# Layer 0's last twelve convolution tiles as six pairs of seven products, with part of the weights' low halves made by accumulating DMAs

## The chip, the cores and the metric

The kernel runs on one core of one Trainium2 chip. The metric is device time in microseconds for one execution. The kernel before took 2328.89 us (median of 3 runs, 2328.8 to 2331.57).

## What is computed

The reference is one inference step of a two-layer trunk, D = 2048, for 128 prompt tokens and 512 sample tokens (640 in all). Each layer normalises x, scales and shifts it by adaLN values (h), multiplies h by one wide input projection, runs two mixers on slices of the result, and adds the output projection's result, gated, to x. Layer 0's second mixer is the short gated convolution of this case:

```python
def gated_short_conv(u, gate_b, gate_c, w):
    z = gate_c * u
    zp = jnp.pad(z, ((0, 0), (1, 1), (0, 0)))
    conv = zp[:, :-2] * w[0] + zp[:, 1:-1] * w[1] + zp[:, 2:] * w[2]
    return gate_b * conv

def modulation(cond, w, b):
    m = jax.nn.silu(cond) @ w + b
    return jnp.split(m, 3, axis=-1)
...
y_b = gated_short_conv(ub, bb, cb, conv_w) * jax.nn.silu(gb)
return jnp.concatenate([y_a, y_b], axis=-1) @ w_out
```

ub, bb, cb and gb are four slices of 1024 columns of the layer's input projection h @ w_in, 6656 columns wide.

## The kernel before

**Numbers.** Every product is made of three matmuls in a rounded 32-bit type: a value is split into a high half (the rounded value) and a low half (the rest), and high by high, high by low and low by high are summed. `split` (lines 240 to 242) makes the high half with an ACT copy and the low half with a DVE subtraction. Weights are loaded as `raw`, 128 x 512 (four blocks of 128 rows of k), and split by `split_w` (line 259) into `wh` and `wl`; there are four buffers each (`W_BUFS`).

**Tiles.** A tile is 128 output columns by all 640 tokens. It goes through sixteen blocks of k in four quarters, and the tokens in two halves of 320 (`proj_q`, lines 270 to 278): 16 x 2 x 3 = 96 matmuls. `run_tiles` runs 52 such tiles for layer 0's input projection. The first six ("leading" tiles) run together while h is made block by block (`h0_maker`, lines 889 to 901; ACT's line 897 writes the high half) and while adaLN weights for layer 0, in 2 MB DMAs, go through TensorE (line 178). The other 46 follow, first those for attention (k, v, q, gates) with the convolution tiles of i = 0 to 3 between them, then sixteen convolution tiles, u, c, b and h for each i = 4 to 7 (`b_tiles`), of which no attention is left beside.

**Slots and fills.** After each quarter `slot` advances a step of attention and, at a given rate, a step of a fill: `ada_on_dve` (lines 194 to 229) computes the other adaLN blocks on DVE, 16 steps a block, each a load of 256 KB and two DVE instructions (line 213). `fill0` does twelve blocks at 1.2 steps a slot.

**Pairs.** `run_pairs` (from line 431) takes two tiles at once as a two-by-two block product (k in halves, tokens in halves) with seven half-tile products, in the order Q1, Q2, N5, P6, P7, P4, Q3. Each product is 8 blocks of k x 3 = 24 matmuls (lines 526 to 528) on sums of weight blocks, formed by `operand` on DVE in a tile `sx` (lines 462, 465, 472), and on sums of token blocks (T1 to T4), formed before by `forms` (lines 1050 to 1074) from the mixer outputs in memory. Weight parts are split three parts ahead (`SPLIT_AHEAD`); a part is half a product, 12 matmuls. Here the pairs serve the output projections alone: `project_out` (line 1098) runs three leading tiles, one single tile, and six pairs for layer 0.

**Order.** Each engine works in its own order, which the tile framework sets when the program is built; buffers and semaphores do the rest. Mixer outputs go to memory by DMAs that POOL issues (line 827), and the residual's transpose too (line 909). SP issues the loads.

Of the kernel before, what the change touches and what calls it, by code (L numbers as in the profile page):

```python
# [15 lines left out]
ALU = mybir.AluOpType  # L16
# [29 lines left out]
SPLIT_AHEAD = 3  # L46
N_FILL0 = 12
FILL0 = 1.2
FILL1 = 0.9
# [4 lines left out]
def trunk_kernel(ctx: ExitStack, tc: tile.TileContext, I: dict, O: dict):  # L54
# [136 lines left out]
    def ada_on_dve(blocks, tags, parts=1, tie=lambda: None):  # L191
# [4 lines left out]
        for l, cb in blocks:  # L196
# [34 lines left out]
            yield  # L231

    ready = set()

# [22 lines left out]

    mark = [None]
# [39 lines left out]

    credit = [0.0]

    def slot(fill=None, rate=0.0):
        advance(prep, len(prep))
        advance(attn, 1)
        credit[0] += rate
        while credit[0] >= 1.0:
            next(fill, None)
            credit[0] -= 1.0

    def run_tiles(jobs, w_ap, make_h, fill=None, rate=0.0, ahead=None, order=(0, 1, 2, 3), before=None,
                  last=None, by_half=False, trans=[], grace=0, cut=None, summed=None, led=None, fill_from=0, lead_in=None):  # L310
        if trans:
            lp = tc.tile_pool(name="lead", bufs=1, side="right")
            lead_pool = lp.__enter__()
            sums = {n: lead_pool.tile([P, NT], F32, name=f"sum{n}") for n in trans}
            held = [n for n in range(2 + len(trans)) if n not in trans]

            leads = [n for m in range(len(held) + 1) for n in trans[m:m + 1] + held[m:m + 1]]
            leads += trans[len(held) + 1:]
        else:
            leads, held, lp = list(range(min(3, len(jobs)))), [], None  # L320
# [4 lines left out]
        for ui, (pos, qd, js) in enumerate(units):  # L325
            raws = {n: load_raw(w_ap, jobs[n][0], qd, js) for n in leads[:W_BUFS]}
# [66 lines left out]
        if before:  # L393
            settle()
        else:
            n = pending.pop(0)
            begin(jobs[n][1], pps[n])
        for i in range(lead, len(jobs)):
# [3 lines left out]
            for qd in range(4):  # L402
                proj_q(pp, parts[t], qd, qd, HV[:1] if split_last else HV)
                if before and qd == 0:
                    before(i)
                t += 1
                run_ahead(t)
                if pending and not prep:
                    n = pending.pop(0)
                    begin(jobs[n][1], pps[n])  # L410
                slot(fill, rate if t > fill_from else 0.0)
            if split_last:
# [17 lines left out]

    def run_pairs(cols, w_ap, mov, room, begin, part, done, tail):

# [22 lines left out]
        def operand(p, name):  # L455
# [3 lines left out]
            if name == "N5":  # L459
                x = st8["x"] = ap.tile([P, W8, P], F32, tag="sx", name="sx", bufs=1)  # L460
                for i in range(2):
                    V.tensor_add(halves(x)[i], halves(a("A21"))[i], a("A22")[i])
                return halves(x)
            if name == "P6":
                V.tensor_add(st8["x"], st8["x"], a("A11"))
# [24 lines left out]
        def after(p, name, ps):  # L490
# [8 lines left out]
            elif name == "P6":  # L499
                V.tensor_sub(u2, ps, q1)  # L500
                V.tensor_sub(u4, st8["n5"], u2)
                if p == len(cols) - 1:
                    part(p, 0, 1, u4)
            elif name == "P7":
                V.tensor_sub(z, ps, u4)
                done(p, 1, 1, z)
                V.tensor_add(u2, ps, u2)
                part(p, 1, 0, u2)
            elif name == "P4":
                done(p, 1, 0, ps)  # L510
            elif p == len(cols) - 1:
                done(p, 0, 1, ps)
# [7 lines left out]
        for i, (p, name) in enumerate(seq):  # L520
            ps, rows_ = pproj.tile([P, 512], F32, tag=f"p{'ab'[i % 2]}{i // 2 % 2}", name="pq")[:, 0:HALF], mov[MOV[name]]
            for h in range(2):
# [6 lines left out]
                if h == 0:  # L529
                    ahead(2 * i + 1)  # L530
                    slot()
            after(p, name, ps)
# [8 lines left out]
            if name in ("P6", "P7") and p == len(cols) - 1:  # L541
                tail(name)
            slot()

# [198 lines left out]
    def pair_gen(ap, width, k, banded, emit, done, sinks):  # L743
# [35 lines left out]
        for u in range(6):  # L779
# [12 lines left out]
            if u < 5:  # L792
# [21 lines left out]
    fill0 = ada_on_dve(ada_rest[:N_FILL0], ("acc0", "acc1", "adaw", "adaw", "adaw", "z"))  # L814
    fill1 = ada_on_dve(ada_rest[N_FILL0:], ("acc0", "acc1", "adaw", "adaw", "adaw", "adaw"), 2,
                       lambda: mark[-1])
# [3 lines left out]
    xdram = [dram.tile([P, NT], F32, name=f"xd{k}") for k in range(KT)]  # L820

# [83 lines left out]
    def keep(ui, n, pp):  # L905
        g = {(4, 0): 0, (4, 4): 1, (5, 0): 2, (5, 4): 3}.get((ui, n))
        if g is not None:
            V.tensor_copy(xTm[g][:, 4 * NT:], pp[1][:, 0:1])
            nc.gpsimd.dma_start(x0dram[g], xTm[g])

    def even_start():
        close("start")
        open_pool("even")


# [98 lines left out]
    for i in range(4):  # L1014
# [29 lines left out]

    def forms():

        f = None

        def load(j):
            ts = [big("w8", bufs=4)[:, 0:NT] for _ in range(2)]  # L1050
            for i in range(2):
                nc.sync.dma_start(ts[i], ydram[j + 8 * i])
            return ts
# [4 lines left out]
        for j in range(8):  # L1058
            (ya, yb), nxt = nxt, (load(j + 1) if j < 7 else None)
            b11, b12, b21, b22 = ya[:, 0:HALF], ya[:, HALF:NT], yb[:, 0:HALF], yb[:, HALF:NT]  # L1060
            x = big("sx")[:, 0:3 * HALF]
# [3 lines left out]
            x2, x3, x4 = (x[:, i * HALF:(i + 1) * HALF] for i in range(3))  # L1065
            V.tensor_sub(x3, b12, b22)
            V.tensor_sub(x2, b11, x3)
            V.tensor_sub(x4, b21, x2)
            V.tensor_sub(d, b11, b12)
            t = big(f"T{j}", dtype=F32R).rearrange("p (s n) -> p s n", s=2)  # L1070
            split(t[:, 0, :], t[:, 1, :], x)
            T.append(t)
# [22 lines left out]
    def form_of(i):  # L1095
        return lambda j: (T[j][:, 0, i * HALF:(i + 1) * HALF], T[j][:, 1, i * HALF:(i + 1) * HALF])

    def project_out(l, maker, finish, last, tail):

        w = W_OUT[l]  # L1100

        def job(n):
            def f(pp):
                res_load(l, n)
                for i in range(2):
                    res_sum(l, n, pp[i], CS[:1] if i == 0 else CS[1:])
                yield
                finish(n)
            return f

        n0 = N_SINGLE[l]
        go_on = run_tiles([(n * P, job(n)) for n in range(3)], w, maker, order=(0, 2, 1, 3))


        quarters = [(n * P, qd) for n in range(3, n0) for qd in range(4)]
        raws, parts = [], []
# [8 lines left out]
        go_on()  # L1125
        for n in range(3, n0):
            pp, t = new_pp((n - 3) % 2), 4 * (n - 3)
            for hv in ([HV] if n < n0 - 1 else [HV[1:], HV[:1]]):
# [10 lines left out]
            while n == n0 - 1 and go_on():  # L1139
                pass  # L1140
            drain(prep)
            prep.append(job(n)(pp))
            advance(prep, 1)

# [13 lines left out]
        def done(p, t, h, src):  # L1158
# [4 lines left out]
            elif n in seen:  # L1163
                prep.append(later(n))
            seen.add(n)

        run_pairs([(n * P, (n + 1) * P) for n in range(n0, KT, 2)], w,
                  {"B11": half_of(0, 0), "T1": half_of(0, 1), "B21": half_of(8, 0), "B22": half_of(8, 1),
                   "T2": form_of(0), "T3": form_of(1), "T4": form_of(2)}, room, begin, part, done, tail)
        drain(prep)  # L1170


    make_y0 = y_maker(("q0h", "q0l", "q1h", "q1l"), NT)
# [60 lines left out]
    def x1_tail(name):  # L1234

        for k in (range(0, 4) if name == "P6" else range(4, 6)):
            x1_back(k, big("w8", bufs=4) if k < 4 else big("sx" if k == 4 else "sf"))

# [3 lines left out]

    project_out(0, y0_maker, x1_done, x1_last, x1_tail)

    def h1_maker(k, hv):
        if k == 0 and hv[0][0] == 0:
            for g in range(3):
                t = big(f"T{g}")
                for i in range(3 if g < 2 else 2):
                    x1_back(6 + 3 * g + i, t, i)  # L1250
            for i in (14, 15):
                x1[i] = st["xr", i]
# [151 lines left out]
    def y1_maker(k):  # L1404
        if k == 4:
# [4 lines left out]
            open_pool("fin")  # L1410
            attn.append(forms())
        if k % 8 >= 4:
# [87 lines left out]
```

## Time and profile before

| | us |
|---|---|
| runs, median (lowest to highest) | 2328.89 (2328.8 to 2331.57) |
| profiled execution, own time | 2333.26 |
| its span | 2331.3 |
| layer 0: start and leading tiles | to about 175 |
| layer 0: tiles beside attention | to about 690 |
| layer 0: last sixteen convolution tiles | to about 912 |
| layer 0: output projection, leading and single tiles | to about 980 |
| layer 0: output projection, pairs | to about 1106 |
| layer 1 | to the end |

In the rows of the profile, PE is TensorE's matmuls, PEld its weight loads, DVE the vector engine, ACT the scalar engine, POOL the engine that also issues DMAs, and SP the one that issues the loads. A row of stretches gives each engine's busy time and its count of instructions, then TensorE's granted clock, the mean busy share of the 16 DMA engines and GB/s. A row of a timeline gives start, duration, engine, line, operation, output and input, and in brackets how long the engine had been idle before it and what ended that. L12 is line 12 of the kernel before.

### The profile page before, as it was taken

What the parts mean: (1) busy time and instruction counts of PE and PEld (TensorE: products, weight loads), DVE (VectorE), ACT (ScalarE), POOL (GpSimd) and SP (SyncE); (2) the same over time, 40 slices, a digit from 0 to 9 for tenths busy, and PEclk for the clock granted to TensorE, in tenths of its full rate; (3) what the DMA queues carried; (4) which work ended last, traced back from release to release, by engine and by line L of the source; (5) the groups of instructions that cost most, each with busy time, mean ns of one, the idle gap of its engine ahead of it and who ended that gap; (6) DMA issues with size and microseconds to landing.
All of it is one profiled execution on the core that took longest, in us unless ns stands there. A gap on an engine that the chain in (4) does not pass through costs nothing.

```text
span 2331.3 us, 41439 instructions
## 1 busy us (share of the span) xinstructions
PE 2286.6 (98%) x15988; PEld 2210.0 (95%) x15988; DVE 1572.5 (67%) x3196; ACT 929.2 (40%) x1935; POOL 133.0 (6%) x181
## 2 busy tenths in 40 slices
PE   7999999999999999999999999999999999999999
PEld 5699999999999999999999999999999999999999
DVE  4559886786876663988855755755756754567576
ACT  4235442433422222544554344444334444444343
POOL 1001000000000000000010100101000001000101
PEclk9999999999999999999999999999999999999999
DMA  9984545445355443844431422413423312128642
GB/s 315 354 267 131 162 116 170 139 119 169 116 180 162 151 139 114 277 142 128 160 98 53 135 82 72 143 52 100 118 72 95 104 46 82 46 74 270 181 122 70
DMA packets 390630, 321.96 MB, mean 138 GB/s; under 512 B 18402, under 2 KB 336368, under 8 KB 389920
## 3 DMA queue, kind: packets, MB, share of 16 engines
q1 hardware_dynamic: 382496, 288.98, 40.9%
q0 software_dynamic: 7216, 28.16, 3.3%
q8 instruction: 126, 2.06, 0.4%
q10 hardware_dynamic: 720, 2.16, 0.3%
q14 instruction: 72, 0.59, 0.1%
HBM read 290.79 MB, written 28.44 MB: 137 GB/s over the span
## 4 chain that ended last, share of the span: by engine, by line
PE 88%; DMA 4%; DVE 4%; ACT 2%; issue 1%; POOL 0%; SPq 0%; ACTq 0%; DVEq 0%; POOLq 0%
PE pa L276 10%; PE pb L277 10%; PE pb L276 10%; PE pb L278 10%; PE pa L277 10%; PE pa L278 10%; PE pq L526 4%; PE pq L528 4%; PE pq L527 4%; PE T L704 2%; PE S L716 1%; PE S L718 1%; PE S L717 1%; DMA yin<-yd 1%; PE T L178 1%
## 5 line engine op out<-in xcount | busy, mean ns | idle before, releaser
L241 ACT ACTIVATE wh<-raw 128x512 fp32r<-128x512 f32 (+1 forms) x490 | 303.1, 620 | 794.7 <-PE pb L277 655.3
L242 DVE TENSOR_TENSOR wl<-raw,wh 128x512 fp32r<-128x512 f32 (+1 forms) x490 | 330.8, 676 | 351.3 <-ACT wh L241 326.1
L276 PE MATMUL pa<-h,wh 128*128 128x320 f32 x1760 | 560.6, 319 | 4.5 <-ACT h L241 3.2
L277 PE MATMUL pa<-h,wh 128*128 128x320 f32 x1760 | 547.3, 312 | 1.8 <-DVE h L242 1.8
L278 PE MATMUL pa<-h,wl 128*128 128x320 f32 x1760 | 546.4, 310 | 0.0
L278 PE MATMUL pb<-h,wl 128*128 128x320 f32 x1760 | 545.4, 310 | 0.0
L276 PE MATMUL pb<-h,wh 128*128 128x320 f32 x1760 | 545.0, 310 | 0.0
L277 PE MATMUL pb<-h,wh 128*128 128x320 f32 x1760 | 544.8, 310 | 0.0
L213 DVE SCALAR_TENSOR_TENSOR acc<-adaw,sT,acc 128x512 f32<-128x512 f32 (+1 forms) x600 | 357.4, 639 | 13.1 <-DMA adaw<-in_ada_w 12.4
L276 PEld LDWEIGHTS pa<-h,wh 128*128 128x128 f32 x1760 | 331.9, 189 | 24.0 <-issue 14.7
L277 PEld LDWEIGHTS pa<-h,wh 128*128 128x128 f32 x1760 | 332.6, 189 | 6.3 <-DVE h L242 2.7
L278 PEld LDWEIGHTS pa<-h,wl 128*128 128x128 f32 x1760 | 332.1, 189 | 1.2 <-issue 1.2
L278 PEld LDWEIGHTS pb<-h,wl 128*128 128x128 f32 x1760 | 330.8, 188 | 2.1 <-issue 2.1
L276 PEld LDWEIGHTS pb<-h,wh 128*128 128x128 f32 x1760 | 330.6, 188 | 1.0 <-issue 0.4
L277 PEld LDWEIGHTS pb<-h,wh 128*128 128x128 f32 x1760 | 330.8, 188 | 0.2
L690 ACT ACTIVATE p<-S,nm,rq 128x768 f32<-128x768 f32 (+3 forms) x120 | 101.2, 844 | 114.8 <-DVE nm L685 81.1
L526 PE MATMUL pq<-h,wh 128*128 128x320 f32 x352 | 110.0, 313 | 0.4 <-DVE xr L1083 0.4
L527 PE MATMUL pq<-h,wh 128*128 128x320 f32 x352 | 108.8, 309 | 0.0
L528 PE MATMUL pq<-h,wl 128*128 128x320 f32 x352 | 108.4, 309 | 0.0
L683 DVE TENSOR_REDUCE nm<-S 128x1 f32<-128x768 f32 (+3 forms) x120 | 91.9, 766 | 16.1 <-PE S L718 14.9
L241 ACT ACTIVATE pth<-T 128x512 fp32r<-128x512 f32 (+1 forms) x132 | 65.9, 533 | 71.4 <-PE T L704 71.3
L527 PE MATMUL pq<-T,wh 128*128 128x320 f32 x264 | 81.4, 308 | 0.0
(303 smaller groups left out, 3382.5 us busy)
## 6 DMA issues: line engine op xcount, KB each, us to landing
raw<-in_od_w_in SPq DMA_DIRECT2D x208, 256.0 KB, 2.8
raw<-in_ev_w_in SPq DMA_DIRECT2D x196, 256.0 KB, 3.0
adaw<-in_ada_w SPq DMA_DIRECT2D x192, 256.0 KB, 3.0
ada<-in_ada_w SPq DMA_DIRECT2D x14, 2048.0 KB, 11.0
adaw<-in_ada_w SPq DMA_DIRECT2D x128, 128.0 KB, 2.3
yd<-y POOLq DMA_DIRECT2D x34, 320.0 KB, 2.8
yin<-yd SPq DMA_DIRECT2D x32, 320.0 KB, 4.8
w<-yd SPq DMA_DIRECT2D x32, 320.0 KB, 4.4
```

The source lines that it names most:

```text
L213: V.scalar_tensor_tensor(out=a, in0=w, scalar=sT[:, kt, c:c + 1], in1=a, op0=ALU.mult, op1=ALU.add)
L241: A.activation(hi, x, AF.Copy)
L242: V.tensor_sub(lo, x, hi)
L276: PE.matmul(ps, wh[:, i, :], hi[:, sl], start=(j == js[0] if alone else (pos == 0 and j == 0)), stop=False)
L277: PE.matmul(ps, wh[:, i, :], lo[:, sl], start=False, stop=False)
L278: PE.matmul(ps, wl[:, i, :], hi[:, sl], start=False, stop=(j == js[1] - 1 if alone else (pos == 3 and j == 3)))
L526: PE.matmul(ps, wh[:, j, :], hi, start=(h == 0 and j == 0), stop=False)
L527: PE.matmul(ps, wh[:, j, :], lo, start=False, stop=False)
L528: PE.matmul(ps, wl[:, j, :], hi, start=False, stop=(h == 1 and j == 3))
L683: V.tensor_reduce(nm, s, axis=AX.X, op=ALU.max, negate=True)
L690: A.activation(p[:, 0:n], s, AF.Exp, scale=rsc, bias=nm, accum_out=l)
L704: PE.transpose(t[:, i * P:(i + 1) * P], p, ident)
```

## The change

- Layer 0's input projection keeps 36 tiles in `run_tiles`. The last sixteen go through a new function `project`, split out of `project_out`: four single tiles (u, c, b, h of i = 4), then twelve tiles in six pairs (u with c, b with h). The pool "even" of attention closes before them, and "mid" opens there instead of inside the output projection.
- The pairs need the token blocks' forms. `whole_tokens` writes h to memory: for each of 16 blocks one DMA of the high half and one accumulating DMA of the low half, all issued on POOL. `forms` takes its source as an argument and works in place.
- `split_w` can leave the subtraction to a DMA: ACT writes the high half, ACT writes its negative into `wl`, and a DMA on POOL adds `raw` to it. Two splits of three go so in the tiles beside attention (`by_dma` = 3), one of two from the convolution tiles to the end of layer 0's output projection (`by_dma` = 2).
- In `run_pairs` N5's sum of weights is formed in place in the loaded block A21, and the sum for P7 is formed at N5 instead of at P6. The convolution's results go through `conv_put`, by token halves.
- `fill0` has ten blocks at 1.64 steps a slot; the two others go by half blocks (`ada_by_half`, two 128 x 256 DVE instructions a step) at 0.42 steps a slot in the new pairs and in layer 0's output pairs.
- The output projection's first four inputs come through the three `xr` buffers (`late_yin`), no longer through four buffers of the old pool.

```diff
-N_FILL0 = 12
-FILL0 = 1.2
+N_FILL0 = 10
+FILL0 = 1.64
+FILL0_PAIRS = 0.42
+FILL0_LATE = 0.42
...
     def split_w(raw):
         wh = wpool.tile(raw.shape, F32R, tag="wh", name="wh")
         wl = wpool.tile(raw.shape, F32R, tag="wl", name="wl")
-        split(wh, wl, raw)
+        turn[0] += 1
+        if by_dma[0] and turn[0] % by_dma[0]:
+            A.activation(wh, raw, AF.Copy)
+            A.activation(wl, wh, AF.Copy, scale=-1.0)
+            nc.gpsimd.dma_start(wl, raw, accum_op=ALU.add)
+        else:
+            split(wh, wl, raw)
...
             if name == "N5":
-                x = st8["x"] = ap.tile([P, W8, P], F32, tag="sx", name="sx", bufs=1)
+                f = st8["f"] = ap.tile([P, W8, P], F32, tag="sf", name="sf", bufs=1)
+                V.tensor_add(f, a("A11"), a("A21"))
+                x = st8["x"] = a("A21")
                 for i in range(2):
-                    V.tensor_add(halves(x)[i], halves(a("A21"))[i], a("A22")[i])
+                    V.tensor_add(halves(x)[i], halves(x)[i], a("A22")[i])
                 return halves(x)
             if name == "P6":
                 V.tensor_add(st8["x"], st8["x"], a("A11"))
-                f = st8["f"] = ap.tile([P, W8, P], F32, tag="sf", name="sf", bufs=1)
-                V.tensor_add(f, a("A11"), a("A21"))
                 return halves(st8["x"])
...
+    def whole_tokens():
+        for _ in range(30):
+            yield
+        for k in range(KT):
+            for s, how in zip(hs[k], ({}, {"accum_op": ALU.add})):
+                nc.gpsimd.dma_start(hdram[k], s, **how)
+                yield
+
     def even_start():
         close("start")
         open_pool("even")
+        by_dma[0] = 3
+        extra.append(whole_tokens())
...
-    for i in range(4, 8):
-        b_tiles(i)
...
+    close("even")
+    open_pool("mid")
...
+    by_dma[0] = 2
+    attn.append(forms(hdram))
+    project(I["ev_w_in"][0], [EV["ucbh"[n % 4]] + (4 + n // 4) * P for n in range(16)], 0, 4, None, conv_job,
+            lambda p: None, None, lambda p, t, h, src: conv_put(4 + 2 * p + t, h, src), lambda name: None,
+            fill_late, FILL0_PAIRS)
...
     def y0_maker(k):
-        if k < 4:
-            return make_y0(k)
         if k == 8:
-            close("even")
-            open_pool("mid")
-            st["acc"] = pools["cur"].tile([P, NT], F32, name="acc")
-            st["sq"] = pools["cur"].tile([P, NT], F32, name="sq")
-            attn.append(forms())
+            attn.append(forms(ydram))
         late_yin(k)
```

More of the change, by code (lines that the diff above doesn't have):

```diff
@@ L297, in drain, with slot @@
             advance(queue, 1)
-    credit = [0.0]
-    def slot(fill=None, rate=0.0):
+    credit, pace, extra = [0.0], [0.0], []
+    def slot(fill=None, rate=0.0, steps=1.0):
         advance(prep, len(prep))
-        advance(attn, 1)
+        advance(extra, 1)
+        pace[0] += steps
+        while pace[0] >= 1.0:
+            advance(attn, 1)
+            pace[0] -= 1.0
         credit[0] += rate
@@ L542, in run_pairs @@
                 tail(name)
-            slot()
+            slot(fill, rate)
     def stage(ap, pp):
@@ L1095, in form_of, with project @@
     def form_of(i):
[L1096 to L1115, printed above, removed]
+        return lambda j: tuple(T[j][:, s, (2 - i) * HALF:(3 - i) * HALF] for s in range(2))
+    def project(w, cols, leads, n0, maker, job, begin, part, done, tail, fill=None, rate=0.0):
+        go_on = run_tiles([(cols[n], job(n)) for n in range(leads)], w, maker, order=(0, 2, 1, 3)) if leads else slot
+        quarters = [(cols[n], qd) for n in range(leads, n0) for qd in range(4)]
         raws, parts = [], []
@@ L1165, in done @@
             seen.add(n)
[L1167 to L1173, printed above, removed]
+        project(W_OUT[l], [n * P for n in range(KT)], 3, n0, maker, job, begin, part, done, tail,
+                *((fill_late, FILL0_LATE) if l == 0 else ()))
```

164 lines of the change are left out of this document (131 added, 33 removed).

## Prediction

> **What bounds the kernel now.** I read the page's busy shares and its chain first, then busy time by stage.
>
> ```profile
> PE 2286.6 (98%) x15988; PEld 2210.0 (95%) x15988; DVE 1572.5 (67%) x3196; ACT 929.2 (40%) x1935; POOL 133.0 (6%) x181
> ...
> q0 software_dynamic: 7216, 28.16, 3.3%
> ...
> PE 88%; DMA 4%; DVE 4%; ACT 2%; issue 1%; POOL 0%; SPq 0%; ACTq 0%; DVEq 0%; POOLq 0%
> ```
>
> ```profile
> 38.00:175.00 137.00, 131.93 (x989) 107.39 (x990) 70.03 (x171) 43.52 (x100) 2.19 (x4) 0.98 0.90 308
> 175.00:690.00 515.00, 512.82 (x3647) 498.39 (x3646) 408.64 (x825) 202.98 (x454) 23.32 (x25) 1.00 0.48 143
> 690.00:897.00 207.00, 207.00 (x1427) 204.57 (x1426) 128.95 (x235) 42.70 (x76) 2.16 (x4) 1.00 0.49 147
> 980.00:1106.00 126.00, 125.56 (x855) 125.13 (x854) 107.69 (x179) 53.32 (x86) 5.40 (x10) 1.00 0.49 143
> ```
>
> The columns are PE, PEld, DVE, ACT, POOL busy time, TensorE clock, DMA share, GB/s. TensorE bounds every stage: layer 0's leading tiles (38 to 175 us), its tiles beside attention (to 690), the convolution tiles that the change takes up (to 897) and the paired output projection (980 to 1106). But the slack differs: in the lead the DMA share is 0.90, so two resources are nearly full; among the last convolution tiles DVE is at 62% and DMA at half.
>
> **The change, part by part.** The sum is made against the profiled execution, 2333.26 us (span 2331.3). The runs' median is 4.4 us lower, and I take 4.4 off at the end.
>
> *Matmuls removed.* A pair of tiles is eight half-tile products of 24 matmuls; seven do now. Six pairs: 6 x 24 = 144 matmuls of 128x320 fewer, which the built program's order confirms (12792 to 12648).
>
> ```profile
> 750.00:800.00 50.00, 50.00 (x346) 49.39 (x346) 34.37 (x62) 9.70 (x18) 0.00 (x0) 1.00 0.54 164
> ```
>
> 50 / 346 = 0.1445 us each: **-20.8 us**, all on the path, if nothing waits.
>
> *Low halves by DMA, in the pairs.* In the built order one weight part in two, always a product's first, gets its low half so: ACT writes the high half, ACT writes its negative, POOL issues a DMA that adds the raw weights. The same part of the old output projection shows the cover. The rows are ACT, then DVE, then PE, at layer 0's pairs; sx is the sum of weight blocks for the products N5 and P6.
>
> ```profile
> 1032.12 0.63 ACT L241 ACTIVATE wh<-sx 128x512 fp32r<-128x512 f32 x1 [1.13 <-PE pq L527]
> 1033.82 0.63 ACT L241 ACTIVATE wh<-sx 128x512 fp32r<-128x512 f32 x1 [0.44 <-PE pq L527]
> ...
> 1034.48 0.69 DVE L242 TENSOR_TENSOR wl<-sx,wh 128x512 fp32r<-128x512 f32 x1 [0.25 <-ACT wh L241]
> 1035.21 1.23 DVE L465 TENSOR_TENSOR sx<-sx,w 128x1024 f32<-128x1024 f32 x1
> 1037.21 0.69 DVE L242 TENSOR_TENSOR wl<-sx,wh 128x512 fp32r<-128x512 f32 x1 [0.78 <-ACT wh L241]
> ...
> 1040.81 0.31 PE L526 MATMUL pq<-T,wh 128*128 128x320 f32 x1
> 1040.95 0.31 PE L527 MATMUL pq<-T,wh 128*128 128x320 f32 x1
> 1041.10 0.31 PE L528 MATMUL pq<-T,wl 128*128 128x320 f32 x1
> ```
>
> At 1032.12 the first part of N5 is split, released by the matmul that gave its buffer back; at 1035.21 DVE adds a block to sx for P6, in place; P6's low half is ready at 1037.90, and TensorE first needs it at 1041.10. The cover is 3.2 us. In the new order that addition must also wait until N5's DMA has read sx, and P6's own low half needs a second DMA. With D for issue to landing: 1032.12 + 0.63 + 0.63 (negative copy, priced as the other ACT row) + D + 1.23 + 0.63 + 0.63 + D, with 0.1 of hand-over, ends at 1036.0 + 2D. It meets 1041.10 if D is 2.55; beyond that TensorE waits **2D - 5.1** in each of 12 pairs (six new, six of the output projection, which now uses the DMAs as well). DVE is in order: behind the waiting addition stand the part's next subtractions and the sums of finished products, and behind those on SP the next weight block's load. Parts outside this chain have 3 parts of 12 matmuls (5.3 us), less two ACT rows: 4 us for D.
>
> No accumulating DMA is in the trace. Its nearest rows are POOL's plain ones (KB each, us to landing):
>
> ```profile
> yd<-y POOLq DMA_DIRECT2D x34, 320.0 KB, 2.8
> ...
> xd<-xr POOLq DMA_DIRECT2D x16, 320.0 KB, 3.6
> ...
> out_y_sample<-ot POOLq DMA_DIRECT2D x15, 256.0 KB, 3.6
> ...
> out_new_c_k<-kg POOLq DMA_DIRECT2D x8, 64.0 KB, 1.9
> ```
>
> On the line through 64 KB and the faster 320 KB, 256 KB land in 2.6 us: the lower end. The accumulation also reads its destination: q0 moved 28.16 MB in 3.3% of 2331 us, 2.73 us per MB, so 0.7 us for another 256 KB, D = 3.3. The upper end is the same-size row plus that, 4.3. I take 3.3, since a second read is real work: 1.5 us a pair, **+18 us** (ends +1 and +42).
>
> The Trainium skill's page "DMA: Bandwidth & Descriptors" (section "Anatomy of one DMA — SWDGE (gpsimd) path") fits a GpSimd-issued DMA as 2.0 us plus its bytes at 436 GB/s, an estimate of 2.6 us here, and says nothing there of an accumulation's second read. By that price the pairs would cost 1 us, and the sum would be 17 lower. The faster row of 320 KB fits it; the same-size row, 3.6, doesn't.
>
> *Copies of h to memory.* 32 DMAs of 320 KB (16 of them accumulating) write the tokens' h for the later forms. The source issues them after 30 slots beside attention; but in the built order they stand first on POOL, ahead of the residual's stores, each waiting only for its h. POOL is empty then, so they run as h is made, in the lead:
>
> ```profile
> L897 ACT ACTIVATE h<-ht,mod x32: 385/558/728, 37.2 to 149.9; 128x512 fp32r<-128x512 f32 x16, 128x128 fp32r<-128x128 f32 x16
> ```
>
> ```profile
> POOL x0d L909 <- DVE xT L908: 129.4, 3, 115.3
> ...
> PE T L178 <- DMA ada<-in_ada_w: 4.3, 2, 3.3
> ```
>
> ```profile
> 38.00:60.00 22.00, 22.00 (x174) 18.98 (x175) 10.22 (x26) 8.81 (x23) 0.00 (x0) 0.92 0.86 298
> 60.00:80.00 20.00, 14.96 (x106) 7.52 (x105) 6.60 (x18) 4.06 (x8) 0.00 (x0) 0.91 1.07 387
> 80.00:105.00 25.00, 25.00 (x172) 17.09 (x171) 13.23 (x29) 6.33 (x12) 0.00 (x0) 1.00 0.92 323
> 105.00:130.00 25.00, 25.00 (x203) 21.43 (x200) 18.02 (x42) 10.79 (x22) 0.00 (x0) 1.00 0.97 309
> 130.00:165.00 35.00, 34.97 (x275) 32.44 (x274) 19.59 (x52) 8.96 (x20) 1.66 (x3) 1.00 0.73 250
> ```
>
> At 2.73 us per MB the 10.5 MB are 29 us of all 16 engines, 43 with the second read. Up to 130 us the engines have 4 us free of 92, and TensorE already waits for ada weights (60 to 80: 5.0 us idle). h 0 to 3, eight copies, 7 to 11 us, fall there: I charge 8. h 4 to 11, sixteen copies, 14 to 21 us, meet loads that run a buffer ahead while TensorE is full: I charge a quarter, 4. The last eight fit the free 9 us after 130. **+12 us**, ends 0 and +28 (everything over the free time).
>
> The same page (section "Issuing engines are not separate DMA queues") says that what POOL issues shares the 16 engines with SP's loads, which speaks against this part: by it the copies press on the lead; with a path of their own they would cost 0 and the sum be 12 lower. No row of before shows such a load beside SP's.
>
> *DVE beside attention.* Ten adaLN blocks go in 30 tiles' 120 slots at 1.64 steps a slot, not 1.2; two of three splits leave DVE.
>
> ```profile
> L213 DVE SCALAR_TENSOR_TENSOR acc<-adaw,sT,acc 128x512 f32<-128x512 f32 x261 | 185.7, 745 | 4.9 <-DMA adaw<-in_ada_w 4.4 <-DVE acc L213 0.4
> L242 DVE TENSOR_TENSOR wl<-raw,wh 128x512 fp32r<-128x512 f32 x118 | 81.2, 688 | 59.3 <-ACT wh L241 53.5 <-PE T L555 5.6
> ...
> 200.00:250.00 50.00, 49.80 (x364) 46.33 (x363) 47.95 (x108) 24.90 (x58) 3.84 (x3) 1.00 0.44 128
> ```
>
> A slot is 515 / 120 = 4.3 us, 11.7 in 50 us, a step two instructions: +0.44 x 11.7 x 2 x 0.745 = +7.6 us of DVE, -0.67 x 11.7 x 0.69 = -5.4. The fullest stretch goes from 47.95 to 50.2 of 50: **+1 us** (0 to +5); elsewhere there is room. ACT gains 80 x 0.63 = 50 us on 203 of 515: hidden. In the pairs DVE (107.69 of 126) loses seven splits a pair, 4.8 us, and gains 64 / 12 = 5.3 half-width ada steps, each two of these:
>
> ```profile
> L213 DVE SCALAR_TENSOR_TENSOR acc<-adaw,sT,acc 128x256 f32<-128x256 f32 x240 | 102.4, 479 | 7.6 <-DMA adaw<-in_ada_w 7.4
> ```
>
> That is 5.1 us, so nothing changes: it stays hidden under TensorE's 168 x 126/855 = 24.8 us a pair, and 3 us more of DVE work there would not.
>
> *Forms and seams.* The new forms' DVE work is eight rounds of four subtractions and a split, priced by the old forms:
>
> ```profile
> L242 DVE TENSOR_TENSOR T<-sx,T 128x960 fp32r<-128x960 f32 x16 | 18.5, 1158 | 3.7 <-ACT T L241 3.5
> ...
> L1068 DVE TENSOR_TENSOR sx<-w,sx 128x320 f32<-128x320 f32 x16 | 7.8, 487 | 0.2
> ```
>
> 8 x (4 x 0.49 + 1.16) = 25 us in the four single tiles' 4 x 96 x 0.1445 = 55, beside eight weight splits (5.5) and the convolution, with no ada: hidden; so are the 16 loads of 320 KB, 14 us of the engines' time at a share of one half. The first output tiles lose their four input buffers and go through three: **+2 us** (0 to +6).
>
> Sum: -20.8 + 18 + 12 + 1 + 2 = **+12**, 2345.5 on the profile's scale, **2341 us** in the runs' median.
>
> **Rivals.**
>
> *The cover holds (faster).* D is near 2.6 and the lead's loads run far enough ahead: -20.8 + 1 + 5 + 1 + 2 = -12, 2317 us. For it: the faster 320 KB row, 2.8, and a lead in which TensorE idles only 5 us of 137. Against: the second read, and a DMA share of 0.95 up to 130 us. It decides at D = 2.9 with a lead of 9: then 8 + 9 + 3 cancels the 20.8.
>
> *The ring of four weight buffers binds.* If D passes 4.3, even parts outside the chain are late: four parts take 7.04 us now; two ACT rows, D and the ten matmuls after the wait are 2.8 + D. At D = 5.3 that is 1.0 us per four parts, 42 times, and the chain's 5.5 a pair overlaps it; some 7 a pair, 84 in all: +78, 2407 us. For it: 3.6 for a plain 256 KB row, with half the engines' time already taken. Against: it needs two thirds more than that line gives.
>
> *Nothing measurable.* The terms cancel, as at the point above: 2329. That the change doesn't remove the matmuls is excluded by their count; that TensorE's time doesn't shrink is the forecast itself.
>
> **How the numbers follow.** A measurement tells about 0.2%, 4.7 us, from no change. Forecast, 2334 to 2382: 0.53. Cover holds, below 2324: 0.27. Nothing: 0.08. Ring, above 2382: 0.12. So slower 0.65, same 0.08, faster 0.27. Own range of the forecast: 2334 to 2382 (D up to 4.3, less a cheaper lead). The range reaches the faster case: 2312 to 2382.
>
> **What would show it.** Matmuls of 128x320 144 fewer and the convolution's stage shorter; POOL rows wl<-raw with a time to landing over 2.6; TensorE idle once a pair before P6's first matmul with a low half, released by a DMA; hd stores between 38 and 165 us and the last leading tile later by some 12 us, with longer ada landings. I am wrong if the DMAs land in 2.6 us or less, if TensorE's rate in the pairs stays at 855 matmuls in 126 us, or if the lead ends at 175 as before.

## The result and the profile after

The changed kernel takes **2475.99 us** (2473.94 to 2479.38, 4 runs) against 2330.23 for the kernel before in the same comparison: a ratio of 1.0627, 95% interval 1.0608 to 1.0645, so **146 us slower**. The forecast was 2341: the sign came true, the size was twelve times too small.

Lines of the changed kernel's page: busy shares; POOL's DMA queue; shares of the chain that ended last; and DMAs with their KB and their median time from issue to landing.

```profile
PE 2323.8 (94%) x15848; PEld 2224.2 (90%) x15848; DVE 1564.9 (63%) x3241; ACT 1067.2 (43%) x2175; POOL 313.7 (13%) x393
...
q0 software_dynamic: 36720, 85.85, 15.9%
...
PE 44%; DMA 4%; DVE 3%; issue 3%; ACT 1%; POOL 0%; POOLq 0%; DVEq 0%; ACTq 0%
...
ada<-in_ada_w SPq DMA_DIRECT2D x14, 2048.0 KB, 13.0
wl<-raw POOLq DMA_DIRECT2D x108, 256.0 KB, 4.3
...
wl<-w POOLq DMA_DIRECT2D x60, 256.0 KB, 4.0
...
hd<-h POOLq DMA_DIRECT2D x32, 320.0 KB, 7.3
```

TensorE's share fell from 98% to 94%, and its busy time rose although 140 fewer matmuls are recorded. The low-half DMAs shown land in 4.0 to 4.3 us (3.3 was taken), the copies of h in 7.3, and the lead's adaLN weights in 13.0 where it was 11.0. Busy time by stage of the changed kernel, in this order: the lead, the tiles beside attention, the convolution's single tiles, its pairs, and five output pairs.

```profile
38.00:205.00 167.00, 139.72 (x976) 109.49 (x977) 67.81 (x167) 44.05 (x95) 28.91 (x40) 0.90 1.02 317
205.00:761.00 556.00, 528.47 (x3694) 509.81 (x3693) 391.87 (x801) 249.62 (x542) 92.33 (x104) 0.98 0.67 177
761.00:825.00 64.00, 60.72 (x402) 60.20 (x401) 50.19 (x105) 28.72 (x48) 7.38 (x10) 0.97 0.87 242
825.00:1017.00 192.00, 165.23 (x1026) 157.88 (x1025) 131.90 (x268) 88.84 (x152) 38.09 (x46) 0.93 0.70 173
1110.00:1263.00 153.00, 134.79 (x848) 130.14 (x848) 82.77 (x140) 71.88 (x122) 34.87 (x44) 0.96 0.72 171
```

TensorE idles in every stage, and its granted clock, the figure behind POOL's busy time, is under 1 in every one. By the stores on POOL (the first key, the last output of attention, the first and the last-but-one residual) the loss against the kernel before grows from +29 us at the end of the lead to +66 behind attention and +94 behind the convolution, although the convolution has 20.8 us less to do, and to +137 behind the output pairs. One output pair takes 30.6 us, not 24.6.

One output pair of the changed kernel shows where the time goes. TensorE waits twice, for the first low halves of N5 and of P6. ACT had taken up N5's part at 1115.00, as soon as its buffer was free, and POOL issued its DMA at 1117.07:

```profile
1122.13 0.42 PE L573 MATMUL pq<-h,wl 128*128 128x320 f32 x1 [1.43 <-DMA wl<-w]
1128.68 0.45 PE L573 MATMUL pq<-T,wl 128*128 128x320 f32 x1 [2.12 <-DMA wl<-w]
```

```profile
1115.00 0.63 ACT L295 ACTIVATE wh<-w 128x512 fp32r<-128x512 f32 x1 [1.13 <-PE pq L572]
...
1117.07 0.85 POOL L297 DMA_DIRECT2D wl<-w  x1 [1.01 <-ACT wl L296]
```

The same kernel's stretches right behind six such waits, of 1.83, 2.46, 1.43, 2.12, 2.40 and 1.84 us:

```profile
828.90:832.50 3.60, 3.59 (x24) 3.52 (x24) 1.78 (x3) 2.22 (x5) 0.42 (x1) 1.00 0.25 72
836.46:840.00 3.54, 3.54 (x13) 3.54 (x14) 2.54 (x5) 0.70 (x2) 0.00 (x0) 0.50 0.34 89
1122.13:1125.60 3.47, 3.47 (x23) 3.47 (x24) 2.87 (x4) 2.10 (x4) 0.13 (x1) 1.00 0.29 93
1128.68:1132.20 3.52, 3.52 (x14) 3.52 (x15) 1.23 (x1) 0.86 (x2) 0.00 (x0) 0.53 0.53 110
...
1221.75:1225.25 3.50, 3.50 (x24) 3.50 (x25) 1.22 (x1) 1.38 (x3) 0.29 (x1) 1.00 0.51 112
1250.43:1253.93 3.50, 3.50 (x17) 3.50 (x18) 1.23 (x1) 1.26 (x2) 0.22 (x1) 0.70 0.58 138
```

Behind the waits of 2.46 and 2.12 us TensorE does 13 or 14 matmuls in 3.5 us, at half the clock, where it otherwise does 23 or 24. So such a stall takes about another 1.5 us after it is over, and TensorE counts as busy in them. But the length of the wait alone doesn't decide it: behind 2.40 us the clock stayed full, behind 1.84 it fell to 0.70. What decides isn't shown. The Trainium skill's page "TensorE: Matmul & The Clock Gate" (section "HAM oscillation — how this bites in real kernels") gives as its rule no idle gaps of TensorE over about 3.4 us; here the clock also fell behind waits of 1.84 and 2.12 us, so the measurement decides.

### The profile page after: what moved, and what is told of

Its sections match the earlier page's. It is cut to its first block, busy times and chain, and to the rows that moved or that the text cites. A ratio compares the mean times of both kernels' runs of the same rounds, so it can differ in the third digit from the quotient of the medians.

```text
span 2473.9 us, 42126 instructions
## 1 busy us (share of the span) xinstructions
PE 2323.8 (94%) x15848; PEld 2224.2 (90%) x15848; DVE 1564.9 (63%) x3241; ACT 1067.2 (43%) x2175; POOL 313.7 (13%) x393
## 4 chain that ended last, share of the span: by engine, by line
PE 44%; DMA 4%; DVE 3%; issue 3%; ACT 1%; POOL 0%; POOLq 0%; DVEq 0%; ACTq 0%
PE pa L312 5%; PE pb L313 5%; PE pb L312 5%; PE pb L314 5%; PE pa L314 4%; PE pa L313 4%; PE pq L573 3%; PE pq L571 2%; PE pq L572 2%; DMA wl<-w 2%; PE T L749 1%; PE S L761 1%; PE S L763 1%; DMA adaw<-in_ada_w 1%; PE S L762 1%
## 5 line engine op out<-in xcount | busy, mean ns | idle before, releaser
L312 PE MATMUL pa<-h,wh 128*128 128x320 f32 x1568 | 504.9, 323 | 11.2 <-DVE sum L385 6.7
L313 PE MATMUL pa<-h,wh 128*128 128x320 f32 x1568 | 492.2, 314 | 4.0 <-DVE h L271 3.8
L312 PE MATMUL pb<-h,wh 128*128 128x320 f32 x1568 | 489.2, 312 | 0.3 <-ACT sum L383 0.3
L313 PE MATMUL pb<-h,wh 128*128 128x320 f32 x1568 | 489.2, 312 | 0.0
L270 ACT ACTIVATE wh<-raw 128x512 fp32r<-128x512 f32 (+1 forms) x346 | 212.0, 615 | 492.3 <-PE pb L313 359.8
L271 DVE TENSOR_TENSOR wl<-raw,wh 128x512 fp32r<-128x512 f32 (+1 forms) x346 | 231.6, 671 | 268.3 <-ACT wh L270 248.6
L312 PEld LDWEIGHTS pa<-h,wh 128*128 128x128 f32 x1568 | 298.8, 191 | 31.5 <-issue 13.2
L313 PEld LDWEIGHTS pa<-h,wh 128*128 128x128 f32 x1568 | 299.7, 191 | 9.5 <-DVE h L271 5.7
L312 PEld LDWEIGHTS pb<-h,wh 128*128 128x128 f32 x1568 | 298.0, 190 | 1.7 <-ACT sum L383 0.6
L313 PEld LDWEIGHTS pb<-h,wh 128*128 128x128 f32 x1568 | 298.0, 190 | 0.6 <-issue 0.4
L571 PE MATMUL pq<-h,wh 128*128 128x320 f32 x544 | 169.8, 312 | 0.0
L572 PE MATMUL pq<-h,wh 128*128 128x320 f32 x544 | 168.8, 310 | 0.0
L297 POOL DMA_DIRECT2D wl<-raw x108 | 94.3, 876 | 518.1 <-ACT wl L296 403.6
L573 PE MATMUL pq<-T,wl 128*128 128x320 f32 x408 | 131.9, 328 | 28.1 <-DMA wl<-w 27.3
L295 ACT ACTIVATE wh<-raw 128x512 fp32r<-128x512 f32 x108 | 67.9, 629 | 198.9 <-PE pb L313 137.6
```

The costliest lines, as they stand in the source:

```text
L270: A.activation(hi, x, AF.Copy)
L271: V.tensor_sub(lo, x, hi)
L295: A.activation(wh, raw, AF.Copy)
L297: nc.gpsimd.dma_start(wl, raw, accum_op=ALU.add)
L312: PE.matmul(ps, wh[:, i, :], hi[:, sl], start=(j == js[0] if alone else (pos == 0 and j == 0)), stop=False)
L313: PE.matmul(ps, wh[:, i, :], lo[:, sl], start=False, stop=False)
```

## The experiments

Each kernel ran beside runs of the kernel before on its chip; the figures in brackets below are against those: the difference where it is given, the ratio, and its 95% interval.

**1. Which part costs what.** Three kernels are built on the changed one. e1 makes all low halves on VectorE, e6 keeps the weight DMAs beside attention alone, and e9 is e6 with a VectorE addition in place of each DMA.

```
- by_dma[0] = 3 ... by_dma[0] = 2        (e1: both 0; e6: the second 0 only)
+ V.tensor_add(wl, wl, raw)              (e9: as e6, in place of the DMA)
```

> The changed kernel, with every low half subtracted on VectorE (no accumulating weight DMA); seven-product pairs, the copies of h in the lead and the denser adaLN steps stay. Theory A (an accumulating DMA lands in 4.3 us plus its issue, its cover is 3 to 4, and each stall it leaves also lowers TensorE's clock for a few us; beside attention its negative copies and its queue hold up the order of ACT and POOL): the pairs return to 24.6 us and the attention stage loses its +37, so only the lead's +29 is left against -20.8: 2335 to 2350 us. Rival B (the attention stage is longer because ten adaLN blocks at 1.64 steps a slot and the fuller DMA engines hold up its steps; the pairs because of the late adaLN steps): VectorE gets more work, not less, and the time stays above 2400 us with VectorE over 95% busy in the pairs.

> The changed kernel with the low halves by DMA beside attention only; from the convolution's singles on, all low halves are on VectorE. Theory A: the convolution's pairs and the output pairs give back what the DMAs cost there (some 50 and 43 us), and the attention stage keeps its +37: 2376 to 2395 us, output pairs every 24.6 to 25.5 us, attention's last tile near 760 us as in the changed kernel. Rival B (the pairs are longer by the half-width adaLN steps on VectorE, 5.3 a pair, and their loads): pairs stay over 28 us, 2440 us or more.

> As the kernel with low halves by DMA beside attention only (2393 us), but there the DMA is replaced by VectorE's addition of the raw weights to the negative copy; ACT still makes both copies. It tells ACT's share from the DMAs'. Theory A (the DMAs cost the 39 us: their landing, the raw buffers they hold against SP's loads, POOL's queue): near the kernel without any such DMA, 2350 to 2365 us. Rival B (50 us of second copies on ACT stand in order ahead of the attention's exponentials): 2380 to 2398 us.

Measured: e1 2354.01 (+23.1; ratio 1.0095, 1.0075 to 1.0116), e6 2393.23 (+62.3; 1.0273, 1.0251 to 1.0294), e9 2353.99 (+20.9; 1.009, 1.0072 to 1.0107). Theory A each time (e1 4 us over its range). The accumulating weight DMAs cost 145.8 - 62.3 = **83 us from the convolution on** and 62.3 - 23.1 = **39 us beside attention**; ACT's second copies alone cost nothing there (e9 against e1). Why beside attention? The views of e6 show SP's longest sums of waits from 205 to 690 us (us, times, longest), VectorE's for the adaLN weights and the engines' busy time from 205 to 735 us, and two of TensorE's waits from 212 to 760 us:

```profile
SPq L283 <- DMA wl<-raw: 183.3, 58, 9.4
SPq L209 <- DVE acc L215: 95.7, 91, 4.3
```

```profile
DVE acc L215 <- DMA adaw<-in_ada_w: 59.3, 38, 3.5
...
DVE acc L213 <- DMA adaw<-in_ada_w: 11.4, 1, 11.4
```

```profile
205.00:735.00 530.00, 500.68 (x3514) 480.85 (x3513) 385.67 (x788) 240.22 (x522) 89.31 (x98) 0.98 0.68 179
```

```profile
PE S L761 <- ACT p L735: 9.8, 4, 5.9
...
PE pa L314 <- DMA wl<-raw: 3.6, 1, 3.6
```

And the same waits in e1:

```profile
SPq L209 <- DVE acc L215: 112.2, 105, 3.0
SPq L283 <- DVE wl L271: 110.4, 89, 5.8
```

```profile
DVE acc L215 <- DMA adaw<-in_ada_w: 5.9, 8, 2.0
...
DVE acc L213 <- DMA adaw<-in_ada_w: 5.0, 1, 5.0
```

In e6 SP waits 183 us for `raw` buffers that a DMA has not yet read; the adaLN weights' loads stand behind on SP, and VectorE, in order, waits 71 us for them (11 in e1) with attention's operations queued behind. TensorE waits 28 us in all in that stretch, for attention's operations above all, and for a low half only once, 3.6 us. The adaLN loads also land later than in e1, in 3.7 us against 3.0; how much of the 39 us comes of that, and not of the order on SP, isn't separated. The next kernel takes these loads away:

```
- FILL0 = 1.64
+ FILL0 = 0.0                            (e15, on e6)
```

> As the kernel with low halves by DMA beside attention only (2393 us), but no adaLN step runs beside attention: all ten blocks are made between attention and the convolution, where TensorE then waits for them, so only the stretch up to attention's last store is read (520 us there, 516 without the DMAs it was with them on VectorE, from the first key's store). Theory A (SP's queue waits for raw buffers that the accumulating DMAs still read, 183 us in 58 waits; the adaLN weights behind them come late, and VectorE, in order, waits 71 us for them with attention's operations behind): without adaLN steps the stretch falls from 548 to 520 us or less. Rival B (what costs is the DMAs' landing ahead of the low matmuls and POOL's queue ahead of the norms' powers): it stays over 535 us.

The whole is 2541.92 (one run), as the blocks are made up later. The stretch from the first key's store (210.05) to attention's last (712.34) takes 502.3 us; in e6 it takes 548.4 (211.79 to 760.15), in e1 515.6. In e15, busy time in it, and SP's wait:

```profile
210.00:712.00 502.00, 500.79 (x3554) 490.69 (x3553) 209.99 (x480) 240.62 (x514) 87.16 (x100) 1.00 0.49 119
```

```profile
SPq L283 <- DMA wl<-raw: 393.3, 76, 10.7
```

SP waits for the DMAs twice as long as in e6, and TensorE idles 1.2 us: theory A. So neither the landing nor POOL's queue costs anything worth naming by itself: the DMAs hurt through the adaLN loads behind them. The run also takes VectorE's own adaLN work away; but in e6 VectorE waited rather than worked (386 of 530 us busy), and in e1, with that work and no weight DMAs, the stretch is 515.6 us against 512.6 before.

**2. The copies of h.** On e1, the copies are held back to the tiles beside attention: each waits for one element that a DMA writes over its place from the newest low half. e3 spends three slots on each of the 16 blocks, e12 goes over all blocks three times (elements, plain copies, accumulating copies), and e14 spends five slots on each block.

```
+ nc.gpsimd.dma_start(hdram[k][0:1, 0:1], mark[0][0:1])
  nc.gpsimd.dma_start(hdram[k], hs[k][0])
  nc.gpsimd.dma_start(hdram[k], hs[k][1], accum_op=ALU.add)
```

> As the first of these kernels (no accumulating weight DMA), and the 32 copies of h are held back to the tiles beside attention: each copy waits for one element written over its place by a DMA that is issued after 30 slots. Theory A (in the lead the copies press on full DMA engines and lengthen it by 29 us; beside attention a third or more of the DMA time is free): the lead ends near 178 us as before the change, and the time is 25 to 32 us under the first of these kernels, 2308 to 2322, some 10 to 20 us under the kernel before. Rival B (10.5 MB written and 5.2 MB read again cost the same wherever they lie, or the held-back POOL queue now delays the powers of the attention's norms): under 10 us less than the first of these kernels, 2330 or more.

> All low halves on VectorE and the copies of h held back to the tiles beside attention as before (2332 us), but the gates, the plain copies and the accumulating ones are issued in three rounds, so that a copy seldom waits on POOL for its gate or its plain copy to land. In the run before, TensorE waited 5.9 us at 420 us for a key's norm whose power stood on POOL behind such a copy. Theory A (the wait in POOL's order is what the copies cost there): the attention stage loses 5 to 10 of its +13 us: 2321 to 2327 us, under the kernel before. Rival B (the copies' bytes, or the denser adaLN steps): 2329 to 2336 us.

> All low halves on VectorE, and the copies of h held back and spread: gate, plain and accumulating copy over five slots for each of 16 h, from the 24th slot on, where 2332 us came with three slots each and 2346 us with all of them together. Theory A (the copies cost beside attention by crowding the adaLN weights' and raw weights' loads, and the less they crowd the less they cost): the attention stage 515 to 520 us where it was 525 and 539, 2322 to 2328 us, 3 to 9 us under the kernel before. Rival B (the cost goes with the bytes, not their density; the order 2332 and 2346 came from single waits that fall elsewhere each time): 2329 to 2340 us.

Measured: e3 2332.25 (1.0002, 0.9992 to 1.0013), e12 2346.3 (1.0056, 1.0041 to 1.0072), **e14 2318.9 (0.996, 0.9946 to 0.9973)**. The lead between 38 and 165 us, in the changed kernel and in e14:

```profile
38.00:165.00 127.00, 106.44 (x762) 78.87 (x762) 53.27 (x125) 32.22 (x70) 20.30 (x28) 0.91 1.05 330
```

```profile
38.00:165.00 127.00, 121.76 (x922) 97.38 (x920) 67.56 (x164) 38.34 (x83) 1.69 (x4) 0.97 0.90 306
```

With the copies the DMA engines are full throughout and TensorE does 160 matmuls fewer in the same time; without them the first key is stored at 181.1 us, as before (181.9), not at 211.3. So the lead's +29 is theirs, as theory A of e3 said. Where they go to matters as much: attention's stretch, by the same stores as above, took 525.4 us in e3, 538.7 in e12 and 517.6 in e14, where e1's took 515.6. That is why e3's whole time is in rival B's range and not in theory A's. e14's stretch is theory A's, its time 3 us under it. e12 missed both theories. It is no clean test. TensorE's largest wait beside attention there, and VectorE's between 310 and 440 us:

```profile
PE pa L314 <- DVE wl L271: 9.2, 6, 2.3
```

```profile
DVE wl L271 <- DMA hd<-wl: 9.2, 6, 3.3
```

That is, my gate, which reads a `wl` buffer, kept VectorE from writing it again. How much of the rest is crowding stays open. e14 is the best version: all of the change but its weight DMAs, with the copies moved and spread, 0.4% under the kernel before.

> As the spread copies, and in each pair the sum for P7 and the sum for N5 are made half by half in turn, so that VectorE has N5's first half ready 0.6 us earlier. Theory A (layer 1, which the change leaves alone but for that order of sums, is 3.4 us longer than before because N5 now waits for P7's full sum, 1.23 us): 1 to 3 us under the run with spread copies. Rival B (no TensorE wait depends on it): the same within 1 us.

```
- V.tensor_add(f, A11, A21); then x = A21 + A22 by halves
+ for each half: f = A11 + A21, then x = A21 + A22
```

2326.44 (0.9978, 0.9968 to 0.9988): not under e14 but 7 us over it in the medians. Theory A is refuted, and rival B's 1 us is missed too, in runs that spread over 9 us; that layer 1 lost 3.4 us by the order of sums was read from one profile, and in e14's profile layer 1 takes 1 us more than before.

**3. The pairs.** Two things can make a low half late. The chain is the row from N5's DMA over the addition in place to P6's DMA. The ring is the four weight buffers: a part can be split only when the buffer of the part four before it is free. On the changed kernel, e4 puts N5's and P6's first low halves on VectorE, e8 does a part's low matmuls last, and e13 does both. e5 makes the DMAs plain, so its low halves are the raw weights.

```
e4:  split_w(..., own = product is N5 or P6)   -> no DMA
e8:  for j: wh x hi, wh x lo;  then for j: wl x hi
e5:  nc.gpsimd.dma_start(wl, raw)              (no accum_op)
```

> The changed kernel, but the first low halves of N5 and P6 (the two ends of the chain through the in-place addition to x) are subtracted on VectorE too; all other accumulating DMAs stay. Theory A (the chain N5 - addition - P6 carries the pairs' loss, 3.5 us of stall and some 2 us of lower clock a pair): the 12 pairs lose 5 us each, 60 in all: 2400 to 2430 us, output pairs every 25 to 26.5 us. Rival B (the ring of four weight buffers or the DMAs' landing binds the other products too): the stalls move to the first low halves of Q1, Q2, P7, P4 or Q3, the pairs stay over 28.5 us, 2445 us or more.

> The changed kernel with the order of a pair's matmuls within each weight part changed: the eight with the high half first, then the four with the low half, so a low half is needed 0.88 us later in its part (six matmuls at 0.1467). Theory A (the ring of four weight buffers, refuted as the lesser cause by nobody yet: a part's buffer comes free four parts before, 5.3 us of matmuls, and two ACT rows, hand-overs and the DMA take some 6.7; a pair then idles 7 x (6.7 - 5.3 - 0.3) / 2 = 3.9 us, and 0.88 more cover leaves 7 x 0.1): stalls in a pair fall under 1.5 us, the lower clock after them goes too, 4 to 5.5 us in each of 12 pairs: 2410 to 2430 us. Rival B (the chain N5 - addition - P6 or VectorE's wait behind it): first low halves of N5 and P6 still idle TensorE 2 us or more a pair, gain under 25: 2450 us or more.

> The changed kernel with both cures in the pairs: N5's and P6's first low halves on VectorE (alone 2460 us) and the low-half matmuls last in each weight part (alone 2451 us). Alone they won 16 and 25 of the 83 us that the low-half DMAs cost from the convolution on. Theory A (two waits of which either keeps a pair long, each with a stretch of lower TensorE clock behind it that only goes when no stall over some 1.4 us is left): together clearly more than the sum, output pairs at 25 to 26.3 us, 2405 to 2425 us. Rival B (independent costs): the sum, 2430 to 2440 us, output pairs at 27 us or more.

> The changed kernel with the weights' low-half DMAs made plain: each overwrites the negative copy with the raw weights, adding nothing (the low half is then the raw weight, so the result is another). Order, waits, bytes written and VectorE's share stay; only the second read and the addition go. Theory A (the accumulation itself makes the landing 4.3 us; a plain one takes 3.5): landing 3.3 to 3.7 us and a time 30 to 55 us lower, 2420 to 2446 us. Rival B (the landing is long by the shared engines and by POOL's slow issue, whatever the DMA does): landing 4.1 or more and a time within 12 us of the changed kernel's 2476.

Measured: e4 2460.13 (1.056, 1.0536 to 1.0583), e8 2450.79 (1.0498, 1.0477 to 1.0519), e13 2425.95 (1.041, 1.0392 to 1.0427), e5 2418.41 (1.0372, 1.0352 to 1.0392). The times of e4 and e8 are rival B's, e8's by 1 us; e4's pairs lie between its theories, and e8's gain is 3 us over rival B's 25. The cures win 17 and 28 us alone, 50 together; e13 is 1 us over theory A's range, e5 2 us under its own. Five output pairs in e4, e8 and e13, one kernel a fence:

```profile
1107.77:1246.55 138.78, 129.30 (x852) 123.64 (x852) 98.97 (x182) 69.16 (x114) 26.26 (x34) 1.00 0.75 184
```

```profile
1085.59:1229.04 143.45, 130.12 (x848) 126.72 (x846) 93.77 (x172) 71.69 (x124) 34.81 (x44) 0.96 0.81 194
```

```profile
1082.99:1210.78 127.79, 126.11 (x850) 123.31 (x849) 97.95 (x182) 67.68 (x114) 26.24 (x35) 1.00 0.78 200
```

27.8, 28.7 and 25.6 us a pair, where the changed kernel took 30.6 and e6, without DMAs there, 25.1. e13's output pairs fell as theory A said, but its reason isn't shown: the gains, 2.8 and 1.9 a pair, give 4.7 as a sum, and 5.0 came. In e4 the waits are on other products' low halves, in e8 on P6's but for one of 1.1 us. So there are **two causes**: the chain, and the ring of four weight buffers. e5: without the second read and the addition the landing falls from 4.3 and 4.0 to 3.4 and 3.0 us, and the time by 60: the accumulation is nearly half of the 122 us that the DMAs cost. The Trainium skill's page "Collectives: The Full Stack" (section "The bandwidth ceiling: the fold count and why AG ≠ RS ≠ AR") puts a ReduceScatter's lower rate, against an AllGather's, down to the two source reads of its add; e5 agrees in direction, but takes the read and the addition away together and doesn't tell them apart.

Each cause by itself, on e1, with DMAs only for N5 and P6 (e17: 24 of them), or only for the other five products (e18: 60):

> Accumulating DMAs only for the first low halves of N5 and P6, two in each of the 12 pairs, and nowhere else; copies of h in the lead as in the changed kernel, so it stands against 2354 us with no weight DMA at all. Theory A (the forecast's chain as it was worked out, a wait of 2D - 5.1 with D at 4.0, the landing of these DMAs in the changed kernel, and a stretch of lower clock behind a stall that long, some 1.5 us): 4.4 us a pair, 53 in all: 2395 to 2412 us, one stall a pair at P6's first low half. Rival B (the chain alone is short of that, since the DMAs now land in less than 3.3 us with POOL and the engines nearly to themselves, and the pairs' loss in the changed kernel comes mainly of the ring): under 20 us, 2358 to 2374 us.

> The complement: accumulating DMAs for the first low halves of the other five products of each pair (60 in all), none for N5 and P6 and none elsewhere; it too stands against 2354 us. Theory A (the ring of four weight buffers alone stalls at some of these, as with the chain on VectorE, where the output pairs took 27.7 us): 2.5 to 3.5 us a pair, 30 to 42 in all: 2384 to 2396 us. Rival B (with N5 and P6 on VectorE and the DMAs landing earlier, nothing is late): under 15 us, 2354 to 2369 us.

Measured: e17 2397.73 (+66.8; 1.0272, 1.0242 to 1.0302), e18 2402.5 (+71.5; 1.03, 1.0278 to 1.0323), against e1's +23.1: the chain 44 us, 3.6 a pair; the ring 48, 4.0 a pair (its theory said 2.5 to 3.5). Both are far over their rivals; e17's time is theory A's, e18's 6 us over it. Together they would be 92; in the changed kernel they are 83 with the single tiles, so they may overlap a little (e17's runs alone spread over 10 us). By the stores, e17 loses 4.4 us a pair to e1 in the convolution and 2.2 in the output projection. The median landing in e17, and two of its waits at P6's first low half, one in the convolution's last pair and one in an output pair:

```profile
wl<-w POOLq DMA_DIRECT2D x24, 256.0 KB, 3.5
```

```profile
948.72 0.41 PE L573 MATMUL pq<-T,wl 128*128 128x320 f32 x1 [3.77 <-DMA wl<-w]
...
1096.59 0.41 PE L573 MATMUL pq<-T,wl 128*128 128x320 f32 x1 [1.87 <-DMA wl<-w]
```

Their DMAs, N5's and P6's, took 3.2 and 5.3 us for the first wait, 3.2 and 4.1 for the second. The longest wait of e17's pairs, 4.35 us at N5's first low half in the convolution's first pair, has another reason too. ACT had the negative copy ready at 785.76, but POOL issued the weight DMA only behind a store of the convolution's output, finished by VectorE at 789.02, that stands ahead of it in POOL's order:

```profile
785.13 0.63 ACT L296 ACTIVATE wl<-wh 128x512 fp32r<-128x512 f32 x1
...
789.32 0.54 POOL L874 DMA_DIRECT2D yd<-yb  x1 [61.19 <-DMA adaw<-in_ada_w]
789.88 0.91 POOL L297 DMA_DIRECT2D wl<-w  x1
```

## Why the prediction failed

- **The removed matmuls, -20.8**: right, as e14 shows in its way: with the two costly parts gone the kernel is 11 us faster; the copies beside attention keep some of the rest (attention's stretch is 517.6 us, 512.6 before).
- **Low halves by DMA in the pairs, +18**: the step that failed most; 83 measured, a few of them in the single and leading tiles, whose DMAs the sum left out. The chain was found, and its formula comes near where each DMA's own landing is put in for D: for the two waits of e17 above, 3.2 + 5.3 - 5.1 = 3.4 (3.77 measured) and 3.2 + 4.1 - 5.1 = 2.2 (1.87). With the median of 3.5 it gives 1.9; e17's waits before P6 were 0.9 to 1.9 us in the output pairs and up to 3.77 in the convolution's. Three things were mis-sized. *D* was 4.0 to 4.3, the upper end, and single landings went over 5: the row of the same size was the better neighbour than the row of the faster kind. *The ring* was put in a rival that "needs two thirds more than that line gives", from D = 4.3 on; it binds at the measured D, so TensorE waits twice a pair, at N5 and at P6, where one wait was forecast. "4 us for D" for parts outside the chain left out the hand-overs and the spread of the landings: in the pair above, ACT takes up N5's part at 1115.00, POOL issues 2.1 us later, where two ACT rows are 1.3, and the DMA lands in 5.0; the 7.1 us stand against 5.3 of three parts of matmuls. *The clock* was left out: behind some stalls TensorE runs at about half rate for 3.5 us, 1.5 us lost. The changed kernel's five output pairs take 153.1 us, of which TensorE is busy 134.8; e6's are busy throughout:

```profile
1047.05:1172.47 125.42, 125.42 (x853) 123.69 (x852) 113.43 (x208) 53.93 (x90) 5.41 (x10) 1.00 0.51 156
```

So of the 27.7 us by which they are longer, 18.3 are idle and 9.4 are slower matmuls, at a mean clock of 0.96.
- **Copies of h, +12**: 29 measured, the upper end ("everything over the free time", +28). The DMA engines were full (a share of 1.05 in the changed lead), and the copies cost about what their bytes take on all 16 engines, 29 us without the second read. A quarter for sixteen copies, because loads run a buffer ahead, was the wrong share. That POOL would issue them in the lead was right.
- **DVE beside attention, +1**: the step was costed by VectorE's busy time, and the low-half DMAs there were put at nothing without a reason; they cost 39 us, by a wait that isn't in the busy time. SP's queue was not followed: the DMA holds the `raw` buffer longer than the subtraction did, and what stands behind that load on SP is VectorE's own input.
- **Forms and seams, +2**: about right. e6's convolution pairs (149.1 us for six) and e14's (148.8) take the 24.8 us a pair that were forecast, and e14's four single tiles 59.7 us where the four after attention took 54.8 before, inside the 0 to +6.

The rival that came nearest is the ring, 2407; the sum of all upper ends, -20.8 + 42 + 28 + 5 + 6 on 2329, would have given 2389. So the sign came true by costs that the sum had small or not at all: it left out the ring, and put the stretch beside attention and the lead at 1 and 12, where 39 and 29 came.

## What to carry to other kernels

A low half, or any small product, made by an accumulating DMA is late by its issue, its queue and the accumulation, so count the cover from the moment that the buffer comes free, for every part and not only for the longest chain. Follow each queue past the waiting instruction to the engine that it feeds: the 39 us beside attention came through VectorE's own loads. Where the DMA engines are nearly full, as at 0.90 in this lead, expect new bytes to cost their full time; and allow for a stall of TensorE its length and up to about 1.5 us more, which some of the stalls of 1.8 us and over cost here and some did not.

## What was not expected of the hardware

- TensorE's granted clock fell to 0.50 and 0.53 for 3.5 us behind waits of 2.46 and 2.12 us and to 0.70 behind 1.84, and stayed at 1.00 behind 2.40, 1.83 and 1.43.
- An accumulating DMA's issue takes POOL longer than that of the same DMA without the addition: 0.86 us in the mean in the changed kernel, 0.53 in e5, each in this order (busy us, mean ns, then idle time):

```profile
L297 POOL DMA_DIRECT2D wl<-w x60 | 51.6, 859 | 214.0 <-ACT wl L296 143.1 <-PE pq L572 29.0 <-DVE wl L271 13.5
...
L297 POOL DMA_DIRECT2D wl<-w x60 | 31.7, 529 | 213.1 <-ACT wl L296 157.3 <-PE pq L572 13.3 <-DVE wl L271 11.4
```

- A copy of 320 KB, half of them accumulating, landed in 7.3 us in the full lead and in 4.4 beside attention (e3).
